# Sum of reciprocals: eight rows of the first 80 computed entirely on ScalarE

## The chip, the cores and the metric

The kernel runs on one core of one Trainium2 chip. The metric is the device time of one execution in microseconds (us). The engines are named as in the profile: PE (TensorE, matmul), DVE (VectorE), ACT (ScalarE), POOL (GpSimd) and SP (SyncE, which here only issues transfers). A profile is of one execution; its span runs from the first to the last instruction of the program.

## The reference

```python
# x: (32, 512, 1024) float32, positive
np.sum(1.0 / x, axis=-1).astype(np.float32)
```

There are 16384 sums of 1024 reciprocals each, over 67.11 MB of input. The output is 64 KB.

## The kernel before

The 16384 sums lie 128 on each of 128 partitions. A "row" r is therefore 128 x 1024 numbers, one sum per partition, 512 KB. Rows 0 to 125 are handled whole; the last two are cut into four half rows, numbered 126 to 129. The rows are loaded into `ring`, which has 40 slots of one row; row r goes into slot r modulo 40, so row r+40 can be loaded only when all readers and writers of row r are done.

The kernel uses 1/a + 1/b = (a + b) / (a b), where a is an element of a row's first half and b the element beside it in the second half. A row thus needs 512 products, 512 reciprocals of products, and a multiply with accumulation. The reciprocal is made on ScalarE as exp(-ln(S a b)), with S = 2^17, which the final multiplication takes out again.

All engines work through one order written out by hand, the list `PLAN` (lines 38 to 73). Each engine runs its own tokens in the order of the list, and each waits only for the data it needs. Semaphore waits come from the recorded reads and writes (`note`, lines 135 to 164). A token is a letter, a row, "+n" for n neighbouring rows, and "@b" for a slot or a bank:

- D n: SP issues the loads of the next n rows (line 187).
- P: POOL multiplies the two halves into `prod`, which has 22 slots of 512 elements (line 199). P0+2 handles two rows in one instruction.
- C and V: for a few rows the product is not POOL's. C copies the row's second half to a PSUM bank through a matmul with the identity (line 209); V multiplies that bank with the first half on DVE (line 220). W is V with both halves from `ring`.
- L: ScalarE takes Ln of the product, in place in `prod` (line 242).
- E: ScalarE takes Exp with scale -1 (line 251). With "@b" the result goes to PSUM bank b, without to `prod` in place.
- S: PE adds the two halves of a row into a PSUM bank, as two accumulating matmuls with the identity (line 232). It is done for about half of the rows, those whose E stays in `prod`.
- R: DVE multiplies and accumulates into the row's column of `sums` (line 267). A row with an S needs 512 elements; a row without needs 1024, its two halves from `ring` against the reciprocal in PSUM. Behind the instruction comes a short one that reads out the accumulator.

A matmul of 32-bit numbers appears in the profile as two passes, two weight loads and two MATMUL instructions.

In the first 80 rows the order repeats with a period of eight rows: POOL makes three pairs of products and a single one, and V makes the eighth, that of row 3, 11, 19, 27, 35, 43, 51, 59, 67 and 75. ScalarE runs L and E on pairs, one instruction of 1024 elements for two rows, alternating Exp to PSUM (banks 6 and 7) and Exp in place. From row 80 on the order is less regular, with many single rows.

When the first 114 sums are all done, they are written out by six transfers (line 289); the rest go out at the end (line 291). One table load at the start (line 84) brings the set that holds both Ln and Exp.

Of the kernel before, what the change touches and what calls it, by code (L numbers as in the profile page):

```python
# [11 lines left out]
def kernel(  # L12
# [5 lines left out]
    nc = tc.nc  # L18
# [5 lines left out]
    R = 40  # L24
    NP = 22
    LAST = F - 2
    DONE = 114
    S = float(2**17)

    PLAN = """
        D2 D10 D14 D14 P0+2 C3@3 S2@0 V3 P2 L0+2@0 C11@3 S3@1 E0+2@6 P4+2 V11 L2+2@2 R0 S6@2
        E2+2 R1 P6+2 L4+2@4 R2 R3 E4+2@6 S7@0 P8+2 L6+2@8 R4 S10@1 E6+2 R5 P10 L8+2@10 R6 R7  # L40
        S11@2 E8+2@6 L10+2@6 R8 E10+2 R9 D11 R10 R11 P12+2 C19@3 S14@0 V19 P14+2 L12+2@12
        S15@1 E12+2@6 S18@2 R12 P16+2 L14+2@16 R13 E14+2 R14 P18 L16+2@18 R15 S19@0 E16+2@6
        P20+2 L18+2@14 R16 S22@1 E18+2 R17 D9 P22+2 L20+2@20 R18 R19 E20+2@6 S23@2 P24+2
        L22+2@0 R20 E22+2 R21 L24+2@2 R22 R23 E24+2@6 P26 C27@3 R24 S26@0 P28+2 V27 R25 D7
        L26+2@4 C35@3 E26+2 S27@1 P30+2 V35 L28+2@8 R26 S30@2 R27 E28+2@6 P32+2 L30+2@10 R28
        S31@0 E30+2 R29 P34 L32+2@12 S34@1 R30 R31 E32+2@6 P36+2 S35@0 L34+2@6 R32 E34+2 R33
        D7 P38+2 S38@2 L36+2@16 R34 R35 E36+2@6 S39@1 P40+2 L38+2@18 R36 C43@3 E38+2 R37 D6
        S42@0 P42 L40+2@14 V43 R38 E40+2@6 P44+2 R39 S43@2 L42+2@20 R40 E42+2 S46@1 R41 D3
        P46+2 L44+2@0 R42 R43 E44+2@6 S47@0 P48+2 L46+2@2 R44 S50@2 E46+2 R45 P50 L48+2@4
        R46 C51@3 R47 E48+2@6 S51@1 P52+2 V51 R48 D6 L50+2@8 C59@3 E50+2 R49 P54+2 S54@0  # L50
        L52+2@10 V59 R50 E52+2@6 R51 S55@2 P56+2 L54+2@12 R52 E54+2 S58@1 R53 D5 P58
        L56+2@16 R54 R55 E56+2@6 S59@0 P60+2 L58+2@6 R56 S62@2 E58+2 R57 D4 P62+2 L60+2@14
        R58 R59 E60+2@6 S63@1 P64+2 L62+2@18 R60 S66@0 E62+2 R61 D4 P66 L64+2@20 R62 C67@3
        R63 E64+2@6 P68+2 S67@2 V67 R64 L66+2@0 S70@1 R65 D4 E66+2 P70+2 L68+2@2 R66 R67
        S71@0 E68+2@6 P72+2 L70+2@4 R68 D3 E70+2 R69 D2 C75@3 P74 L72+2@10 S74@2 R70 V75
        P76+2 E72+2@6 R71 S75@1 L74+2@8 R72 D2 E74+2 R73 D2 P80 S78@0 L76+2@12 R74 P81
        L80@16 R75 S79@2 E76+2@6 P78+2 L81@17 R76 D2 S81@1 E80@5 E81 R80 L78+2@6 W82 E78+2
        R81 R77 D1 D1 D1 D1 D1 P88 C85@6 S85@1 R78 P83 L88@18 V85 E88@7 R79 P84 S84@0
        L82+2@14 R88 E82+2@5 P86+2 L84+2@19 R82 D1 E84+2 R83 D1 D1 D1 C90@7 P91 L86+2@0
        S91@2 R85 P93 V90 E86+2@5 R84 P92 S90@1 L90+2@2 R87 L93@21 W89 L92@10 R86 D1 D1 D1  # L60
        D1 E93@7 P94 S97@0 E92@6 R93 E90+2 P97 S94@3 L89@11 R92 E89@7 P95 L97@8 R91 S95@4
        E97 R90 L94+2@4 W96 R97 P101 C99@6 L96@9 R89 E94+2 S100@0 P98 V99 E96@5 L101@12 R95
        P100 S99@1 L98@13 R96 E101@7 L99+2@16 R101 E98@6 P104 C103@5 R94 E99+2 S105@2 R98
        P102 L104@18 V103 E104@7 W105 L102+2@6 R100 P107+2 C106@6 L105@14 R104 E102+2@4
        S108@0 V106 E105 R102 L106+3@19 P109 S107@3 R103 P110 E106+3 R105 S106@4 R99 P111+2
        L109+2@0 R107 S112@1 R108 E109+2@6 R106 L111+2@10 P114 R109 S111@0 E111+2 R110 P113
        L114@15 R111 C115@7 P116 L113@2 R112 E114@6 V115 E113@5 S117@0 P117 R114 L116@3
        L115@8 P118 E116@7 R113 S118@1 E115@6 P119 L117+2@12 R116 E117+2 R115 P120 S120@2
        L119@9 R117 P121 L120@4 S121@3 R118 E119@7 E120 R119 P122 L121@5 S122@0 E121 R120
        P123 L122@18 R121 E122 W124 L123@6 R122 L124@7 W125 S125@1 E123@7 E124@6 R123 P126  # L70
        L125@14 P127 L126@16 S127@0 R124 E125 P128 L127@17 S128@2 E126@7 P129 R125 E127
        S129@3 L128@19 R126 L129@20 E128 R127 E129 R128 R129
    """.split()

    Ln = mybir.ActivationFunctionType.Ln
    Exp = mybir.ActivationFunctionType.Exp
# [36 lines left out]
    def place(r):  # L113
        if r < LAST:
            return r, 0, H
        part, q = divmod(r - LAST, F - LAST)
        return LAST + q, part * H, H // 2
# [6 lines left out]
    left = set(range(DONE))  # L124
    bank, copied, halves, summed = {}, {}, set(), set()

    history = {}
    begun = {}
    count = {}
# [1 line left out]
    def note(engine, inst, reads=(), writes=()):  # L135
        inst = inst.ins
        known = dict(begun.get(engine, {}))
        before = {}
        for spaces, writing in ((reads, False), (writes, True)):
            for space in spaces:  # L140
                for other in history.get(space, ()):
                    if writing or other[3]:
                        before[other[0].name] = other
        needed = sorted(before.values(), key=lambda o: -o[4])
        for other in needed:
            o_inst, o_engine, o_tick, _, _, o_known = other
            if o_engine == engine:
                continue
            if o_tick <= known.get(o_engine, 0):
                tc.declare_no_dep(inst, o_inst, reason="implied by other waits")  # L150
                continue
            for e, t in o_known.items():
                known[e] = max(known.get(e, 0), t)
            known[o_engine] = max(known.get(o_engine, 0), o_tick)
        count[engine] = count.get(engine, 0) + 1
        begun[engine] = known
        entry = (engine, count[engine])
        if engine == "SP":
            entry = (f"load {count[engine]}", 1)
        for spaces, writing in ((reads, False), (writes, True)):  # L160
            for space in spaces:
                history.setdefault(space, []).append(
                    (inst, *entry, writing, sum(count.values()), known)
                )
# [10 lines left out]
    def slots(r, n):  # L175
        return [("slot", pslot[q]) for q in range(r, r + n)]

    with tc.manual_schedule():
        for op, r, n, b in ops:
# [60 lines left out]
            elif op == "L":  # L240
                pg = prod[:, p : p + n, : place(r)[2]]
                inst = nc.scalar.activation(out=pg, in_=pg, func=Ln, scale=S)  # L242
                note("ACT", inst, writes=slots(r, n))
            elif op == "E":
                pg = prod[:, p : p + n, : place(r)[2]]
                rc = pg
                if b is not None:
                    rc = ps[:, b : b + n, : place(r)[2]]
                    for j in range(n):
                        bank[r + j] = b + j  # L250
                inst = nc.scalar.activation(out=rc, in_=pg, func=Exp, scale=-1.0)  # L251
                if b is None:
                    note("ACT", inst, writes=slots(r, n))
                else:
                    banks = [("bank", b + j) for j in range(n)]
                    note("ACT", inst, slots(r, n), banks)
            elif op == "R":
                q, at, w = place(r)
                other = ps[:, bank[r], :w]
                if r in halves:  # L260
                    row = prod[:, p, :w]
                else:
                    row = ring[:, q % R, at : at + 2 * w]
                    row = row.rearrange("p (h e) -> p h e", h=2)
                    other = other.unsqueeze(1).to_broadcast([P, 2, w])
                total = sums[:, q : q + 1]
                inst = nc.vector.tensor_tensor_reduce(  # L267
                    out=row,
                    in0=row,
                    in1=other,  # L270
                    scale=S,
                    scalar=total if q in summed else 0.0,
                    op0=mult,
                    op1=add,
                    accum_out=total,
                )
                summed.add(q)
                note(
                    "DVE",
                    inst,  # L280
                    [("bank", bank[r])],
                    slots(r, 1) if r in halves else rows(r, 1),
                )

                left.discard(r)
                if not left:
                    for c in range(0, DONE, DONE // 6):
                        part = slice(c, min(c + DONE // 6, DONE))
                        nc.sync.dma_start(out=out_v[:, part], in_=sums[:, part])
                    left.add(-1)  # L290
        nc.sync.dma_start(out=out_v[:, DONE:], in_=sums[:, DONE:])


# [28 lines left out]
```

## Time and profile before

| | us |
|---|---|
| median of 3 runs (168.28 to 168.44) | 168.35 |
| span of the profiled execution | 166.3 |
| what lies around the span, by the median | 2.05 |
| busy in that span: PE | 132.5 |
| busy: ACT | 132.3 |
| busy: DVE | 128.3 |
| busy: POOL | 128.2 |
| one row product on POOL, of a pair (128x1024) / single (128x512) | 2.36 / 1.28 |
| DVE: product 128x512, sum of 128x1024, sum of 128x512 | 0.68, 1.22, 0.68 |
| ACT: Ln or Exp, 128x1024 / 128x512 / 128x256 | 1.05 / 0.62 / 0.40 |

The profile gives no total for the profiled execution other than its span, so the 2.05 us come from the median of the runs. The transfers moved 67.26 MB, 404 GB/s over the span, and up to 441 GB/s in the slices of the first half. Durations are those of single instructions; since the next instruction starts before the last one's end is acknowledged, the distance from start to start ("pitch") is shorter than the duration, unless one needs the other's result. A chain of waits ("the chain that ended last") follows the last instruction back to what released it at each step. Idle time is shown ahead of the instruction that ends it, with what released that one. Instructions of the trace can be matched to tokens, since each engine runs them in the order of `PLAN`.

### The profile page before, as it was taken

The numbers are of one execution on the slowest core, as the hardware profiler recorded it, in microseconds if no ns is written. First come the engines' busy times: TensorE is split into PE (matmuls) and PEld (weight loads), VectorE is DVE, ScalarE is ACT, GpSimd is POOL, SyncE is SP. The second block draws the span as 40 slices with busy tenths as digits, with TensorE's granted clock in tenths as the row PEclk, the third lists the DMA queues.
The fourth block names the chain that finished last, engine by engine and source line by source line (L and its number), as shares of the span: only waits on it lengthen the run. The fifth ranks groups of instructions, "written<-read, shape, count | busy, mean of one in ns | idle before, by whom it ended". The sixth has DMA issues, their size and how long they took to land.

```text
span 166.3 us, 1348 instructions
## 1 busy us (share of the span) xinstructions
PE 132.5 (80%) x292; PEld 55.2 (33%) x292; DVE 128.3 (77%) x282; ACT 132.3 (80%) x157; POOL 128.2 (77%) x81
## 2 busy tenths in 40 slices
PE   0000799978855999999999999988699979989982
PEld 0000333333312444444343433324234424433351
DVE  0000119885787699898998898989899999999994
ACT  3040073949995899999799999996999999999992
POOL 1500795069995999999999999948977869999860
PEclk9999999999996999999999999999999999999999
DMA  5999999999998989999999999999999999999940
GB/s 189 536 394 394 441 441 441 441 441 441 441 441 349 509 368 446 430 417 438 441 434 434 406 426 446 429 424 424 414 437 437 414 410 428 410 409 410 400 139 4
DMA packets 5768, 67.26 MB, mean 404 GB/s; under 512 B 1536, under 2 KB 1536, under 8 KB 3200
## 3 DMA queue, kind: packets, MB, share of 16 engines
q1 hardware_dynamic: 5760, 67.18, 95.6%
q8 instruction: 2, 0.03, 0.1%
q14 instruction: 6, 0.05, 0.1%
HBM read 67.11 MB, written 0.07 MB: 404 GB/s over the span
## 4 chain that ended last, share of the span: by engine, by line
DMA 57%; PE 18%; ACT 8%; DVE 6%; POOL 6%; issue 3%; SPq 1%; ACTq 0%; POOLq 0%; DVEq 0%
DMA ring<-in_x_dram 57%; PE ps L232 15%; POOL prod L199 6%; ACT prod L242 4%; PE ps L209 3%; ACT ps L251 2%; DVE ring L267 2%; DVE prod L267 2%; ACT prod L251 2%; DVE prod L220 1%; SPq L187 1%; DVE sums L267 0%; ACTq L242 0%; POOLq L199 0%; DVEq L317 0%
## 5 line engine op out<-in xcount | busy, mean ns | idle before, releaser
L199 POOL TENSOR_TENSOR prod<-ring 128x1024 f32<-128x1024 f32 (+2 forms) x75 | 127.5, 1727 | 33.5 <-DMA ring<-in_x_dram 27.1
L232 PE MATMUL ps<-ring,ident 128*128 128x512 f32 (+1 forms) x260 | 116.9, 596 | 5.2 <-DVE sums L267 4.5
L242 ACT ACTIVATE prod<-prod 128x1024 f32<-128x1024 f32 (+2 forms) x78 | 68.5, 892 | 24.9 <-DVE prod L220 14.3
L267 DVE CUSTOM_DVE_ANT_1 ring<-ring,ps 128x1024 f32<-128x1024 f32 (+1 forms) x65 | 76.4, 1208 | 8.9 <-ACT ps L251 8.7
L232 PEld LDWEIGHTS ps<-ring,ident 128*128 128x128 f32 x260 | 49.2, 193 | 71.7 <-issue 51.6
L267 DVE CUSTOM_DVE_ANT_0 prod<-prod,ps 128x512 f32<-128x512 f32 (+1 forms) x63 | 40.9, 677 | 0.4 <-PE ps L232 0.4
L209 PE MATMUL ps<-ring,ident 128*128 128x512 f32 x32 | 19.3, 689 | 25.7 <-DMA ring<-in_x_dram 24.0
L251 ACT ACTIVATE ps<-prod 128x1024 f32<-128x1024 f32 (+2 forms) x41 | 34.1, 838 | 4.5 <-DVE sums L267 3.7
L251 ACT ACTIVATE prod<-prod 128x1024 f32<-128x1024 f32 (+3 forms) x37 | 34.4, 931 | 0.9
L220 DVE TENSOR_TENSOR prod<-ring,ps 128x512 f32<-128x512 f32 x16 | 10.9, 684 | 26.3 <-PE ps L209 26.3
L209 PEld LDWEIGHTS ps<-ring,ident 128*128 128x128 f32 x32 | 6.0, 213 | 36.0 <-issue 21.4
L267 DVE DVE_READ_ACCUMULATOR2_ANT sums<- 128x1 f32 x130 | 10.7, 82 | 0.0
L220 DVE TENSOR_TENSOR prod<-ring 128x512 f32<-128x512 f32 x6 | 4.1, 688 | 0.1
L84 ACT ACT_TABLE_LOAD x1 | 1.3, 1283 | 0.7 <-PEq L306 0.7
L267 DVE CUSTOM_DVE_ANT_0 prod<-prod,ps,sums 128x256 f32<-128x256 f32 x2 | 0.9, 475 | 0.0
masks.py:197 POOL MEMSET ident<- 128x128 f32 x1 | 0.2, 204 | 0.3 <-POOLq L306 0.3
masks.py:199 POOL TENSOR_SCALAR_AFFINE_SELECT ident<-ident 128x128 f32<-128x128 f32 x1 | 0.3, 292 | 0.1
L306 POOL MEMSET const-float32-0.0<- 128x1 f32 x1 | 0.1, 98 | 0.2 <-issue 0.2
L306 POOL MEMSET const-bfloat16-1.0<- 128x1 bf16 x1 | 0.1, 101 | 0.0
L306 POOL MEMSET const-uint8-127<- 128x1 uint8 x1 | 0.1, 101 | 0.0
L306 POOL MEMSET const-float32-1.0<- 128x1 f32 x1 | 0.1, 98 | 0.0
## 6 DMA issues: line engine op xcount, KB each, us to landing
ring<-in_x_dram SPq DMA_DIRECT2D x2, 7168.0 KB, 41.2
ring<-in_x_dram SPq DMA_DIRECT2D x2, 3584.0 KB, 29.3
ring<-in_x_dram SPq DMA_DIRECT2D x2, 3072.0 KB, 31.9
ring<-in_x_dram SPq DMA_DIRECT2D x3, 2048.0 KB, 34.0
ring<-in_x_dram SPq DMA_DIRECT2D x1, 5632.0 KB, 30.3
ring<-in_x_dram SPq DMA_DIRECT2D x5, 1024.0 KB, 31.8
ring<-in_x_dram SPq DMA_DIRECT2D x1, 5120.0 KB, 16.5
ring<-in_x_dram SPq DMA_DIRECT2D x1, 4608.0 KB, 30.7
```

The lines of the kernel that those rows point to most:

```text
L84: nc.scalar.add_instruction(mybir.InstLoadActFuncSet(name=nc.get_next_instruction_name(), act_func_set_id=act_sets.index("natural_log_exp_ ...
L187: inst = nc.sync.dma_start(out=ring[:, a : a + m, at : at + 2 * w], in_=x_v[:, q : q + m, at : at + 2 * w],)
L199: inst = nc.gpsimd.tensor_tensor(out=prod[:, p : p + m, :w], in0=ring[:, a : a + m, at : at + w], in1=ring[:, a : a + m, at + w : at + 2 * w],
L209: inst = nc.tensor.matmul(ps[:, b, : place(r)[2]], lhsT=ident, rhs=xs(r, 1), start=True, stop=True,)
L220: inst = nc.vector.tensor_tensor(out=prod[:, p, :w], in0=xs(r, 0), in1=in1, op=mult)
L232: inst = nc.tensor.matmul(ps[:, b, : place(r)[2]], lhsT=ident, rhs=xs(r, h), start=h == 0, stop=h == 1,)
L242: inst = nc.scalar.activation(out=pg, in_=pg, func=Ln, scale=S)
L251: inst = nc.scalar.activation(out=rc, in_=pg, func=Exp, scale=-1.0)
L267: inst = nc.vector.tensor_tensor_reduce(out=row, in0=row, in1=other, scale=S, scalar=total if q in summed else 0.0, op0=mult, op1=add, acc ...
L306: nc = _bacc.Bacc("TRN2", target_bir_lowering=False, num_devices=1)
```

## The change

Rows 11, 19, 27, 35, 43, 51, 59 and 67 get two new tokens on ScalarE. A takes Ln of the row's 1024 elements, in place in its ring slot. Z takes Exp with scale -1 of the same 1024 elements, in place, with an accumulated sum (`accum_out`) into the row's column of `sums`. For these rows C, S, V and R are dropped (eight of each). The L and E of the pair that such a row was in become instructions of one row; A and Z stand right behind that E. The remaining tokens and their order, and those of the loads, stay as they were. Four of the eight replacements in the order:

```
C11@3 ... V11 ... S11@2 E8+2@6 L10+2@6 R8 E10+2 R9 D11 R10 R11
    -> E8+2@6 L10@6 R8 E10 A11 Z11 R9 D11 R10
C19@3 ... V19 ... S19@0 ... L18+2@14 R16 S22@1 E18+2 R17 ... R18 R19
    -> L18@14 R16 S22@1 E18 A19 Z19 R17 ... R18
V27 R25 D7 L26+2@4 C35@3 E26+2 S27@1 P30+2 ... R26 ... R27
    -> R25 D7 L26@4 E26 A27 Z27 P30+2 ... R26
S67@2 V67 R64 L66+2@0 S70@1 R65 D4 E66+2 P70+2 ... R66 R67
    -> R64 L66@0 S70@1 R65 D4 E66 A67 Z67 P70+2 ... R66
```

The rest of the diff, its core:

```diff
         for other in needed:
             o_inst, o_engine, o_tick, _, _, o_known = other
-            if o_engine == engine:
-                continue
             if o_tick <= known.get(o_engine, 0):
                 tc.declare_no_dep(inst, o_inst, reason="implied by other waits")
+                continue
+            if o_engine == engine:
                 continue
...
+            elif op == "A":
+                q, at, w = place(r)
+                row = ring[:, q % R, at : at + 2 * w]
+                inst = nc.scalar.activation(out=row, in_=row, func=Ln)
+                note("ACT", inst, writes=rows(r, 1))
+            elif op == "Z":
+                q, at, w = place(r)
+                row = ring[:, q % R, at : at + 2 * w]
+                inst = nc.scalar.activation(
+                    out=row,
+                    in_=row,
+                    func=Exp,
+                    scale=-1.0,
+                    accum_out=sums[:, q : q + 1],
+                )
+                summed.add(q)
+                note("ACT", inst, writes=rows(r, 1) + [("sum", q)])
+                left.discard(r)
...
-                    slots(r, 1) if r in halves else rows(r, 1),
-                )
-
+                    (slots(r, 1) if r in halves else rows(r, 1)) + [("sum", q)],
+                )
                 left.discard(r)
-                if not left:
-                    ...
+            if not left:
+                ...
```

The first part of it lets a dependency on an earlier instruction of the same engine be declared as implied where other waits already cover it. The last part records which column of `sums` an R writes, and moves the test for the first 114 sums out of R's branch, so that a Z can be the last of them too.

More of the change, by code (lines that the diff above doesn't have):

```diff
@@ L38 @@
     PLAN = """
[L39 to L72, printed above, removed]
+        D2 D10 D14 D14 P0+2 C3@3 S2@0 V3 P2 L0+2@0 S3@1 E0+2@6 P4+2 L2+2@2 R0 S6@2 E2+2 R1 P6+2
+        L4+2@4 R2 R3 E4+2@6 S7@0 P8+2 L6+2@8 R4 S10@1 E6+2 R5 P10 L8+2@10 R6 R7 E8+2@6 L10@6 R8
@@ new lines @@
+        E10 A11 Z11 R9 D11 R10 P12+2 S14@0 P14+2 L12+2@12 S15@1 E12+2@6 S18@2 R12 P16+2 L14+2@16
+        R13 E14+2 R14 P18 L16+2@18 R15 E16+2@6 P20+2 L18@14 R16 S22@1 E18 A19 Z19 R17 D9 P22+2
+        L20+2@20 R18 E20+2@6 S23@2 P24+2 L22+2@0 R20 E22+2 R21 L24+2@2 R22 R23 E24+2@6 P26 R24
+        S26@0 P28+2 R25 D7 L26@4 E26 A27 Z27 P30+2 L28+2@8 R26 S30@2 E28+2@6 P32+2 L30+2@10 R28
+        S31@0 E30+2 R29 P34 L32+2@12 S34@1 R30 R31 E32+2@6 P36+2 L34@6 R32 E34 A35 Z35 R33 D7
+        P38+2 S38@2 L36+2@16 R34 E36+2@6 S39@1 P40+2 L38+2@18 R36 E38+2 R37 D6 S42@0 P42
@@ new lines @@
+        L40+2@14 R38 E40+2@6 P44+2 R39 L42@20 R40 E42 A43 Z43 S46@1 R41 D3 P46+2 L44+2@0 R42
+        E44+2@6 S47@0 P48+2 L46+2@2 R44 S50@2 E46+2 R45 P50 L48+2@4 R46 R47 E48+2@6 P52+2 R48 D6
+        L50@8 E50 A51 Z51 R49 P54+2 S54@0 L52+2@10 R50 E52+2@6 S55@2 P56+2 L54+2@12 R52 E54+2
+        S58@1 R53 D5 P58 L56+2@16 R54 R55 E56+2@6 P60+2 L58@6 R56 S62@2 E58 A59 Z59 R57 D4 P62+2
+        L60+2@14 R58 E60+2@6 S63@1 P64+2 L62+2@18 R60 S66@0 E62+2 R61 D4 P66 L64+2@20 R62 R63
+        E64+2@6 P68+2 R64 L66@0 S70@1 R65 D4 E66 A67 Z67 P70+2 L68+2@2 R66 S71@0 E68+2@6 P72+2
@@ new lines @@
+        L70+2@4 R68 D3 E70+2 R69 D2 C75@3 P74 L72+2@10 S74@2 R70 V75 P76+2 E72+2@6 R71 S75@1
+        L74+2@8 R72 D2 E74+2 R73 D2 P80 S78@0 L76+2@12 R74 P81 L80@16 R75 S79@2 E76+2@6 P78+2
+        L81@17 R76 D2 S81@1 E80@5 E81 R80 L78+2@6 W82 E78+2 R81 R77 D1 D1 D1 D1 D1 P88 C85@6
+        S85@1 R78 P83 L88@18 V85 E88@7 R79 P84 S84@0 L82+2@14 R88 E82+2@5 P86+2 L84+2@19 R82 D1
+        E84+2 R83 D1 D1 D1 C90@7 P91 L86+2@0 S91@2 R85 P93 V90 E86+2@5 R84 P92 S90@1 L90+2@2 R87
+        L93@21 W89 L92@10 R86 D1 D1 D1 D1 E93@7 P94 S97@0 E92@6 R93 E90+2 P97 S94@3 L89@11 R92
@@ new lines @@
+        E89@7 P95 L97@8 R91 S95@4 E97 R90 L94+2@4 W96 R97 P101 C99@6 L96@9 R89 E94+2 S100@0 P98
+        V99 E96@5 L101@12 R95 P100 S99@1 L98@13 R96 E101@7 L99+2@16 R101 E98@6 P104 C103@5 R94
+        E99+2 S105@2 R98 P102 L104@18 V103 E104@7 W105 L102+2@6 R100 P107+2 C106@6 L105@14 R104
+        E102+2@4 S108@0 V106 E105 R102 L106+3@19 P109 S107@3 R103 P110 E106+3 R105 S106@4 R99
+        P111+2 L109+2@0 R107 S112@1 R108 E109+2@6 R106 L111+2@10 P114 R109 S111@0 E111+2 R110
+        P113 L114@15 R111 C115@7 P116 L113@2 R112 E114@6 V115 E113@5 S117@0 P117 R114 L116@3
@@ L73 @@
+        L115@8 P118 E116@7 R113 S118@1 E115@6 P119 L117+2@12 R116 E117+2 R115 P120 S120@2 L119@9
+        R117 P121 L120@4 S121@3 R118 E119@7 E120 R119 P122 L121@5 S122@0 E121 R120 P123 L122@18
+        R121 E122 W124 L123@6 R122 L124@7 W125 S125@1 E123@7 E124@6 R123 P126 L125@14 P127
+        L126@16 S127@0 R124 E125 P128 L127@17 S128@2 E126@7 P129 R125 E127 S129@3 L128@19 R126
+        L129@20 E128 R127 E129 R128 R129
     """.split()
@@ L281 @@
                     [("bank", bank[r])],
-                    slots(r, 1) if r in halves else rows(r, 1),
+                    (slots(r, 1) if r in halves else rows(r, 1)) + [("sum", q)],
                 )
                 left.discard(r)
-                if not left:
[L287 to L290, printed above, removed]
+            if not left:
+                for c in range(0, DONE, DONE // 6):
+                    part = slice(c, min(c + DONE // 6, DONE))
+                    nc.sync.dma_start(out=out_v[:, part], in_=sums[:, part])
+                left.add(-1)
         nc.sync.dma_start(out=out_v[:, DONE:], in_=sums[:, DONE:])
```

## The prediction

> **What bounds the kernel now.** I read the page first, then the busy time by stage, then the instructions of ScalarE in order of time, then the waits of the stages. Two lines of the page, shares of the span by engine and the chain that ended last:
>
> ```profile
> PE 132.5 (80%) x292; PEld 55.2 (33%) x292; DVE 128.3 (77%) x282; ACT 132.3 (80%) x157; POOL 128.2 (77%) x81
> ...
> DMA 57%; PE 18%; ACT 8%; DVE 6%; POOL 6%; issue 3%; SPq 1%; ACTq 0%; POOLq 0%; DVEq 0%
> ```
>
> The averages separate nothing, and the chain gives the loads 57%, so stages are needed. The busy time by stage cuts at 54.50 (row 26 begins on ScalarE), 98.57 (row 68 begins) and 163.30 (ScalarE's last end); columns are busy us and (count) for PE, weight loads, DVE, ACT and POOL, then TensorE clock, DMA share, GB/s. The third line is DVE's last stretch, from the sum of row 76 (R76) to its last sum:
>
> ```profile
> 54.50:98.57 44.07, 43.62 (x102) 18.54 (x100) 39.78 (x86) 42.28 (x42) 43.98 (x22) 1.00 0.99 424
> 98.57:163.30 64.73, 58.43 (x136) 24.46 (x134) 62.33 (x140) 62.17 (x89) 53.68 (x40) 1.00 0.95 393
> 109.22:164.02 54.80, 48.28 (x114) 20.53 (x112) 53.93 (x120) 51.65 (x77) 43.40 (x34) 1.00 0.93 383
> ```
>
> From 54.50 on ScalarE is busy 42.28 of 44.07 us and then 62.17 of 64.73: every stretch that it gains or loses is felt. DVE is at 90% in the first stage and at 53.93 of 54.80 in its last. Who ScalarE waits for, after 54 us, and DVE, after 109 (total us, times, longest):
>
> ```profile
> ACT prod L242 <- DVE prod L220: 3.8, 4, 2.4
> ACT prod L242 <- POOL prod L199: 1.6, 2, 1.3
> ```
>
> ```profile
> DVE ring L267 <- ACT ps L251: 1.5, 2, 0.8
> ```
>
> The instructions of ScalarE in order of time (start, duration) give the pitches used below: the first four lines are a pair L26+2, E26+2, then L28+2, E28+2; the last are single rows (L121, E121, L122, E122):
>
> ```profile
> 54.50 1.06 ACT L242 ACTIVATE prod<-prod 128x1024 f32<-128x1024 f32 x1 [2.44 <-DVE prod L220]
> 55.59 1.06 ACT L251 ACTIVATE prod<-prod 128x1024 f32<-128x1024 f32 x1
> 56.55 1.04 ACT L242 ACTIVATE prod<-prod 128x1024 f32<-128x1024 f32 x1
> 57.62 1.03 ACT L251 ACTIVATE ps<-prod 128x1024 f32<-128x1024 f32 x1
> ...
> 155.27 0.62 ACT L242 ACTIVATE prod<-prod 128x512 f32<-128x512 f32 x1
> 155.92 0.63 ACT L251 ACTIVATE prod<-prod 128x512 f32<-128x512 f32 x1
> 156.46 0.61 ACT L242 ACTIVATE prod<-prod 128x512 f32<-128x512 f32 x1
> 157.10 0.63 ACT L251 ACTIVATE prod<-prod 128x512 f32<-128x512 f32 x1
> ```
>
> An instruction that needs the one before it starts 1.08 later at 1024 elements and 0.65 at 512; one that does not, 0.96 and 0.54 later.
>
> **Part 1, what is removed beside the path.** Per special row one copy (C, one product of two PE passes), one half sum (S, two such), one product and one sum on DVE go. In the chain 28 passes take 12.02 us, 0.43 each, so PE gives back 6 x 0.43 = 2.6 us a row. On DVE a product and a half-row sum have a pitch of 0.60 and 0.61, so 1.2 us a row. I price both at nothing in themselves: between 54.50 and 98.57 the only idle time of ScalarE is ended by DVE's product, never by a sum, so an earlier sum releases nobody. The chain's 18% on PE runs from 51.6 to 79.1 and ends in just such a product. POOL keeps its 75 products (2.35 a pair, 1.28 a single) and was ahead of ScalarE all along (P26 ends at 52.97 before L26 at 54.50, P66 at 94.12 before L66 at 96.52). If POOL's lead were gone, ScalarE would lose up to the 1.5 to 2.4 us of it; but a slower ScalarE lengthens it.
>
> **Part 2, waits that vanish.** L26, L50 and L66 waited for the product on DVE of their second row, 2.44, 0.83 and 0.29 us; without it L50 and L66 give back their 1.12 us. L26 is worked out with the start, next.
>
> **Part 3, ScalarE's new work.** Before, a pair costs 1.08 + 0.96 = 2.04. After, its place holds L (0.65 to E), E (0.54 to A), A of 1024 (1.08 to Z, which needs it) and Z of 1024 (0.96 to the next): 3.23, so +1.19 a special row. In place on the ring, A and Z have the shape of the prod<-prod 128x1024 rows, 1.06 us. What no row of the trace shows is Z's accumulated sum on ScalarE. From below: DVE's sums come with an accumulator read of 82 ns that starts together with the next instruction, so it adds 0 to the pitch. From above: ScalarE's smallest instructions, 128x256, have a pitch of 0.31. I take 0.15, half of that: less than 256 elements' time, but ScalarE need not hide it as DVE does. So 1.34 a special row, between 1.19 and 1.50. By the page "ScalarE: Activation LUTs" of the Trainium skill (section What ACT_TABLE_LOAD costs) an activation takes 186 ns + 0.833 ns per element and overlaps the next by 93 ns. An estimate from this, with one element, is 0.09 for the read and 1.28 a row, which would lower the sum by 0.4. Tables add nothing: Ln and Exp alternate already behind a single load.
>
> **Part 4, by rows.** Row 11 is hidden: ScalarE then waits until P12 ends at 37.05 (2.39 idle), and without V11 it gets to rows 4 to 10 earlier. Row 19: L18 stays at 43.78; E18 44.43, A19 44.97, Z19 46.05, L20 47.16 (was 45.82), then three pairs of 2.04, so L26 at 53.29, past P26's end of 52.97: 1.21 earlier than 54.50. The idle 2.44 has paid for row 19 and gives 1.21 besides. Then six rows (27, 35, 43, 51, 59, 67) at 1.34 add 8.04. ScalarE starts L68 later by 8.04 - 1.21 - 1.12 = **5.7 us** (4.8 with the lower price, 6.7 with the upper).
>
> **Part 5, what is given back.** After row 68 the program is the same, and so a delay can only shrink. ScalarE's recoverable idle there is 2.0 (1.34 before L88, the rest in pieces of 0.09 to 0.25). DVE has less: R76 waits for E76 (0.83), so it starts late by the whole 5.7, and from there to its end DVE idles 54.80 - 53.93 = 0.87. The saving of part 1 on DVE lies ahead of R76, where it waits for ScalarE; it can't be carried over. So the last sum ends 5.7 - 0.9 = **4.8 us** later, between 3.9 and 5.8.
>
> **Part 6, the loads.** Row 51's slot is now freed by Z11, and so on. The chain view shows the cover:
>
> ```profile
> 2.11 49.45 DMA ring<-in_x_dram
> ...
> 101.96 35.20 DMA ring<-in_x_dram
> ```
>
> The first four loads land by 51.56, while the fifth is issued at 35.13: 16 us early, the least lead of the loads that wait for a slot. The one issued at 101.96 lands at 137.16, behind a queue. Slots come at most some 6 us later, so the stream doesn't run dry; price nothing, and beyond 16 us one for one. The other edit, which drops waits of an engine on itself that other waits imply, also counts nothing: no stall in the views is ended by the engine itself.
>
> **Sum.** The profiled execution has a span of 166.3 us; the median of the runs is 168.35, so 2.05 lie around the span, kept as they are. Span 166.3 + 4.8 = 171.1; time 168.35 + 4.8 = **173.2 us**; bounds 172.2 to 174.2.
>
> **A rule for the change, weighed.** DVE's 90% against ScalarE's 96% in the stage that is changed says that the work moves to the fuller engine. The Trainium skill, "Perfetto Trace Analysis", section Optimizing Scalar/DVE Operations, says that with DVE saturated, offloading some work to Scalar may make sense. Here its condition fails by those rows; by the rule the sums above would come out as a gain of up to the 1.2 us a row, 7 us of DVE, which no wait in that stage asks for.
>
> **The rivals.**
> 1. *The stream sets the end (not slower).* If the late stage is paced by the loads alone, the delay is swallowed and the time stays at 168.3. For it: DMA 57% of the chain, DMA share 0.99, and P123 starts at 156.22 on the heels of its load. A pair costs ScalarE 2.04 where the stream gives two rows in 2.4. Against: it decides only if both ScalarE and DVE have 5.7 us to give after row 68, and they have 2.0 and 0.9. The Trainium skill, "Perfetto Trace Analysis", section Roofline, calls elementwise work memory-bound at almost any intensity, with some 435 GB/s for a core's 16 DMA engines. By that rule the time would not move; 424 GB/s between 54 and 99 agrees on the bandwidth, the full ScalarE speaks against the conclusion. 5%.
> 2. *ScalarE's idle is what counts, and the accumulated sum is free.* 4.8 - 2.0 = 2.8 later, 171.1. It needs DVE to have 2 us of hidden slack; 0.87 says no. 8%.
> 3. *Z and the sums on DVE hold each other up,* since both write the tile of sums: each Z waits for the sum then running on DVE, up to its 1.22, half on average. 6 x 0.61 = 3.7 more: 176.9. The code gives the columns separately, and the trace has no such pair of writers. 9%.
>
> That the eight rows are not really moved can't be: their tokens are gone from the order.
>
> **How the numbers follow.** Forecast 173.2: 78%; rivals 5, 8 and 9%. The range reaches from just above rival 2 to some way towards rival 3, 171.9 to 175.2, leaving out rival 1, rival 3 and most of rival 2. A difference of 0.2%, 0.34 us, is about what a measurement of this kernel can tell from none. Faster 0.02, same 0.03 (rival 1 splits), slower 0.95.
>
> **What would show it.** After: ScalarE without a gap from L26 at about 53.3 to the end; busy time up by about 8 x (1.19 to 1.5) = 10 to 12 us, to 142 to 144; L68 near 104.3; PE busy about 20 and DVE about 10 lower; DVE waiting for ScalarE in the first 100 us; R76 to the end nearly unbroken, near 54 us; loads landing as before. It would be wrong if the last stage took under 53 us from R76 on, if ScalarE waited for DVE after row 68, or if Z were far from 1.06 us.

## The result, and the profile after

The changed kernel takes 177.16 us (176.38 to 177.89) against 168.39 us in the same measurement: slower, ratio 1.0526 (95% interval 1.048 to 1.0572). I had forecast slower, 173.2 us with 175.2 at most; 177.16 lies outside. Its runs fall at two levels, 176.4 and 177.9 us; the profile is of a run of 176.47, with a span of 174.7, and what adds 1.4 us in the others no trace here shows.

Two lines of the page, busy time by engine and the chain that ended last:

```profile
PE 120.6 (69%) x244; PEld 48.4 (28%) x244; DVE 122.3 (70%) x258; ACT 141.7 (81%) x181; POOL 129.2 (74%) x81
...
DVE 37%; ACT 26%; DMA 19%; issue 12%; POOL 4%; SPq 0%; DVEq 0%
```

ScalarE has 9.4 us more work and PE 11.9 less, but DVE only 6.0 less, where by the pitches of part 1 8 x 1.21 = 9.7 had been taken off it. The chain no longer rests on the loads: DVE and ScalarE carry 63% of it. The stages, cut at the same instructions as before (L26 to L68, L68 to ScalarE's last end, then R76 to the last sum):

```profile
53.14:103.53 50.39, 36.51 (x67) 13.41 (x66) 35.81 (x76) 49.53 (x61) 49.79 (x25) 0.87 0.99 425
103.53:171.21 67.68, 59.14 (x134) 25.11 (x134) 64.72 (x134) 61.98 (x90) 50.24 (x37) 0.97 0.84 346
114.18:171.94 57.76, 49.38 (x114) 21.16 (x112) 57.75 (x120) 51.46 (x77) 42.14 (x32) 0.97 0.80 326
```

In the first stage ScalarE has no gap (49.53 of 50.39; the rest is 0.03 us ahead of each dependent instruction). In the last line DVE is busy all the time, 57.75 of 57.76, but that is 3.8 us more than the 53.93 which the same instructions needed before. Who waits, on ScalarE after 54 us and on DVE after 113:

```profile
ACT ps L236 <- DVE sums L270: 3.2, 2, 2.8
ACT prod L227 <- DVE prod L205: 1.6, 3, 1.0
ACT prod L227 <- POOL prod L184: 0.3, 1, 0.3
```

```profile
DVE ring L270 <- ACT ps L236: 0.8, 1, 0.8
```

ScalarE now waits for DVE in the late stage, by my own list a sign that I am wrong. The instructions of ScalarE show what a special row costs (L26, E26, A27, Z27, the read of the accumulator, L28):

```profile
53.14 0.61 ACT L227 ACTIVATE prod<-prod 128x512 f32<-128x512 f32 x1
53.78 0.63 ACT L236 ACTIVATE prod<-prod 128x512 f32<-128x512 f32 x1
54.32 1.04 ACT L245 ACTIVATE ring<-ring 128x1024 f32<-128x1024 f32 x1
55.39 1.06 ACT L250 ACTIVATE ring<-ring 128x1024 f32<-128x1024 f32 x1
56.36 0.19 ACT L250 ACTIVATION_READ_ACCUMULATOR ring<-ring 128x1 f32 x1
56.45 1.04 ACT L227 ACTIVATE prod<-prod 128x1024 f32<-128x1024 f32 x1
```

The read of the accumulator is an instruction of its own, 186 ns long, but L28 starts 0.09 us behind it. L26 to L28 is 3.31 where a pair takes 2.04, 1.27 a row. L68 starts at 103.53, 4.96 later than before.

Then the part that I had not seen. The products on DVE, grouped by what they read (count, then minimum, median and maximum in ns, then first and last start), before and after:

```profile
L220 DVE TENSOR_TENSOR prod<-ring,ps x16: 679/684/689, 19.9 to 148.4; 128x512 f32<-128x512 f32 x16
L220 DVE TENSOR_TENSOR prod<-ring x6: 681/688/693, 111.5 to 158.7; 128x512 f32<-128x512 f32 x6
```

```profile
L205 DVE TENSOR_TENSOR prod<-ring,ps x8: 676/678/689, 19.9 to 156.6; 128x512 f32<-128x512 f32 x8
L205 DVE TENSOR_TENSOR prod<-ring x6: 686/978/2826, 116.5 to 166.5; 128x512 f32<-128x512 f32 x6
```

The products with both halves from the ring (the W tokens) took 0.69 us each before; now one takes 2.83. Its place on DVE, and POOL at the same time:

```profile
116.47 2.83 DVE L205 TENSOR_TENSOR prod<-ring 128x512 f32<-128x512 f32 x1
119.22 0.67 DVE L270 CUSTOM_DVE_ANT_0 prod<-prod,ps 128x512 f32<-128x512 f32 x1
```

```profile
116.39 2.35 POOL L184 TENSOR_TENSOR prod<-ring 128x1024 f32<-128x1024 f32 x1
```

W82 starts 0.08 us after POOL's P86+2 and ends at 119.30, 0.55 us after P86+2's end at 118.74. The three others in the middle do the same: W89 ends at 130.39 (P101 at 129.84), W96 at 135.68 (P104 at 135.13), W105 at 145.42 (P111+2 at 144.87), each 0.55 later. Before, five of the six W lay in gaps of POOL, and W124 met only the last 0.13 us of P123, at no cost. W82, for instance, ran from 111.51 to 112.20, between P78+2 (to 110.06) and P88 (from 112.85):

```profile
111.51 0.69 DVE L220 TENSOR_TENSOR prod<-ring 128x512 f32<-128x512 f32 x1
```

```profile
107.69 2.37 POOL L199 TENSOR_TENSOR prod<-ring 128x1024 f32<-128x1024 f32 x1
112.85 1.27 POOL L199 TENSOR_TENSOR prod<-ring 128x512 f32<-128x512 f32 x1 [2.79 <-DVE sums L267]
```

(The view puts P88's wait down to a sum on DVE that ended at that moment; by the order P88 needs no such sum, but its load, which landed at 112.72.) POOL follows the loads, whose landings have hardly moved (row 129 at 161.53, before 161.27); DVE follows ScalarE and came 5 us later. So the W slid out of POOL's gaps and into its products.

The sum, against the profiled spans: L68 later by 4.96; the W longer by 2.14, 0.55, 0.04 and 1.55, together 4.28; idle time of DVE given back, 1.33, taken from start to start (0.73 of it ahead of R82, where the view shows 0.64); so the last sum ends 7.91 later (171.93 against 164.02). The closing of the program behind the last store's landing takes 1.33 us instead of 0.86. 7.91 + 0.47 = 8.4 = 174.7 - 166.3.

### The profile page after: what moved, and what is told of

Same layout as the page of the kernel before. It is cut to its first block, busy times and chain, and to the rows that moved or that the text cites. A ratio compares the mean times of both kernels' runs of the same rounds, so it can differ in the third digit from the quotient of the medians.

```text
span 174.7 us, 1233 instructions
## 1 busy us (share of the span) xinstructions
PE 120.6 (69%) x244; PEld 48.4 (28%) x244; DVE 122.3 (70%) x258; ACT 141.7 (81%) x181; POOL 129.2 (74%) x81
## 4 chain that ended last, share of the span: by engine, by line
DVE 37%; ACT 26%; DMA 19%; issue 12%; POOL 4%; SPq 0%; DVEq 0%
DVE ring L270 20%; DMA ring<-in_x_dram 19%; DVE prod L270 10%; ACT ps L236 9%; ACT prod L227 8%; DVE prod L205 5%; POOL prod L184 4%; ACT ring L245 4%; ACT prod L236 3%; ACT ring L250 2%; DVE sums L270 1%; SPq L172 0%; DVEq L319 0%
## 5 line engine op out<-in xcount | busy, mean ns | idle before, releaser
L217 PE MATMUL ps<-ring,ident 128*128 128x512 f32 (+1 forms) x228 | 112.8, 645 | 30.7 <-DVE sums L270 22.9
L227 ACT ACTIVATE prod<-prod 128x1024 f32<-128x1024 f32 (+2 forms) x78 | 65.0, 846 | 23.7 <-DVE prod L205 12.2
L217 PEld LDWEIGHTS ps<-ring,ident 128*128 128x128 f32 x228 | 45.5, 207 | 98.3 <-issue 52.4
L270 DVE CUSTOM_DVE_ANT_0 prod<-prod,ps 128x512 f32<-128x512 f32 (+1 forms) x55 | 35.9, 676 | 0.9 <-PE ps L217 0.9
L236 ACT ACTIVATE prod<-prod 128x1024 f32<-128x1024 f32 (+3 forms) x37 | 31.0, 840 | 0.9
L194 PE MATMUL ps<-ring,ident 128*128 128x512 f32 x16 | 9.5, 675 | 18.2 <-DMA ring<-in_x_dram 17.8
L205 DVE TENSOR_TENSOR prod<-ring,ps 128x512 f32<-128x512 f32 x8 | 5.4, 680 | 19.9 <-PE ps L194 19.9
L194 PEld LDWEIGHTS ps<-ring,ident 128*128 128x128 f32 x16 | 2.9, 204 | 22.4 <-issue 19.7
L250 ACT ACTIVATE ring<-ring 128x1024 f32<-128x1024 f32 x8 | 8.5, 1057 | 0.3
L205 DVE TENSOR_TENSOR prod<-ring 128x512 f32<-128x512 f32 x6 | 8.4, 1397 | 0.0
L245 ACT ACTIVATE ring<-ring 128x1024 f32<-128x1024 f32 x8 | 8.3, 1040 | 0.0
L250 ACT ACTIVATION_READ_ACCUMULATOR ring<-ring 128x1 f32 x8 | 1.5, 186 | 0.0
```

Source lines behind the costliest of these rows:

```text
L194: inst = nc.tensor.matmul(ps[:, b, : place(r)[2]], lhsT=ident, rhs=xs(r, 1), start=True, stop=True,)
L205: inst = nc.vector.tensor_tensor(out=prod[:, p, :w], in0=xs(r, 0), in1=in1, op=mult)
L217: inst = nc.tensor.matmul(ps[:, b, : place(r)[2]], lhsT=ident, rhs=xs(r, h), start=h == 0, stop=h == 1,)
L245: inst = nc.scalar.activation(out=row, in_=row, func=Ln)
L250: inst = nc.scalar.activation(out=row, in_=row, func=Exp, scale=-1.0, accum_out=sums[:, q : q + 1],)
L270: inst = nc.vector.tensor_tensor_reduce(out=row, in0=row, in1=other, scale=S, scalar=total if q in summed else 0.0, op0=mult, op1=add, acc ...
```

## The experiments

Theory 1: ScalarE's added time delays DVE against POOL, and the rest of the loss is DVE's two-ring products held up by POOL's. Its rivals: the loss is ScalarE's and the long W are a symptom; the work spared on PE and DVE matters; the other edits matter. The kernel before, measured beside each group of them, took 168.24 to 168.28 us by its medians.

**1. The four W from PSUM.** In the changed kernel:

```diff
-S81@1   ... W82  ... S91@2 ... W89  ... S97@0 ... W96  ... C103@5 ... W105
+S81@1 C82@3 ... V82 ... S91@2 C89@3 ... V89 ... S97@0 C96@5 ... V96 ... C103@5 C105@4 ... V105
```

> The changed kernel, but DVE's four products with both halves from the ring in the middle of the late stage (W82, W89, W96, W105) read their second half from a PSUM bank, copied by PE (C and V in place of W). Theory 1, DVE's two-ring product and a POOL product do not run beside each other: in the changed kernel these four took 2.83, 1.23, 0.73 and 2.23 us where 0.69 is usual; from PSUM they take 0.68 each. L68 still starts 4.96 us later than in the kernel before, DVE gives back its 0.88 of idle time, the last sum ends 4.1 us later, time 168.4 + 4.1 = 172.5 us (172.0 to 173.0). Theory 2, the longer time comes from ScalarE's late stage or from the sums, and the long products are a symptom of waits: they stay long or their time turns up elsewhere, 176 to 178 us.

Measured 173.52 us, ratio 1.0304 (1.0279 to 1.0329). All four take 0.69 us and the long ones have gone: theory 1 in kind. It is 0.5 us above my 173.0; in the profile V82 waited 1.32 us for its copy, which PE had to make behind S81, and experiment 2 takes that wait away.

**2. The same, copy of row 82 earlier.** `S79@2 C82@3` instead of `S81@1 C82@3`:

> The changed kernel with W82, W89, W96 and W105 read from PSUM as before, but the copy of row 82 stands one half sum earlier on PE (C82 ahead of S81). In the run with the later copy V82 waited 1.32 us for PE, and the last sum was 5.06 us later than in the kernel before. Theory 1: without that wait the remainder of my sum is left, 4.96 - 0.64 - 0.24 = 4.1 us on the last sum, 172.3 to 172.8 us. Theory 2: the 5.06 are the price of ScalarE's work and the wait was idle anyway: 173.5 us as before.

Measured 173.07 us (172.76 to 173.40), ratio 1.0286 (1.0272 to 1.03). The products now read (minimum, median, maximum in ns; the two left are W124 and W125):

```profile
L208 DVE TENSOR_TENSOR prod<-ring,ps x12: 680/682/690, 19.9 to 152.8; 128x512 f32<-128x512 f32 x12
L208 DVE TENSOR_TENSOR prod<-ring x2: 678/722/766, 161.5 to 162.8; 128x512 f32<-128x512 f32 x2
```

L68 starts 5.00 later, R82 4.72, the last sum 4.19: 5.00 less the 0.87 of part 5 is 4.13, so that part's sum holds within 0.1 once the collisions are gone. The median is 0.3 above the expected interval, of which the longer closing (0.48) is the reason I can name. Against theory 2, the last sum ends 0.87 us earlier than in experiment 1, so the wait of V82 had cost time; that is by one profile of each, and the medians differ by 0.45 us with intervals that overlap.

**3. The kernel before, with the same four from PSUM.**

> The kernel before, with the same four products read from PSUM. In that kernel each of them lies in a gap of POOL and takes 0.69 us. Theory 1: nothing to gain, 168.4 us (168.2 to 168.8), PE busy up by 4 x 0.86 = 3.4 us. Theory 2 (the copy through PE has a price or a gain of its own): different from 168.4 by over 0.5 us, which would then also be in the run of the changed kernel with PSUM.

Measured 168.47 us, ratio 1.0017 (1.0001 to 1.0034); PE busy 135.8 against 132.5. Where the W met no product of POOL, moving them gains nothing.

**4. Collisions without any added work.** In the kernel before, two tokens of DVE change places:

```diff
-L90+2@2 R87 L93@21 W89 L92@10
+L90+2@2 W89 R87 L93@21 L92@10
```

> The kernel before with one token moved: W89 ahead of R87 instead of behind it on DVE. No work is added. W89 then starts at about 121.65, inside POOL's P92 (121.40 to 122.68). Theory 1: W89 ends 0.55 us after P92, at 123.2, DVE is 0.98 us late; W96 then starts at 129.0 inside P101 (128.71 to 129.99) and ends near 130.5, 0.9 us more; W105 starts near 138.1 inside P107+2 (137.29 to 139.66) and ends near 140.2, 1.5 us more. DVE has 0.2 us of idle time left, so the last sum is some 3 us later: 171.5 us (170.5 to 172.5). Theory 2: a swap of two independent instructions on DVE costs nothing, 168.4 us.

Measured 172.48 us (171.03 to 172.81), ratio 1.023 (1.0182 to 1.0278). W89 on DVE, and POOL's P92, which began before it:

```profile
121.71 1.57 DVE L222 TENSOR_TENSOR prod<-ring 128x512 f32<-128x512 f32 x1
123.20 1.21 DVE L269 CUSTOM_DVE_ANT_1 ring<-ring,ps 128x1024 f32<-128x1024 f32 x1
```

```profile
121.45 1.28 POOL L201 TENSOR_TENSOR prod<-ring 128x512 f32<-128x512 f32 x1
```

W89 ends 0.55 after P92. It makes W96 late (1.62 us), that W105 (2.14), and W124, which I had not foreseen, takes 1.27. The four together are 3.85 us longer, each moving DVE into the next one, and DVE also waits 1.2 us for half sums of PE, where it waited for none in that stretch before. The last sum is 4.73 us later, with the same instructions in the kernel.

**5. ScalarE's time alone.** In the kernel before, six tokens stand twice (E28+2@6, E36+2@6, E44+2@6, E52+2@6, E60+2@6, E64+2@6), the second writing what the first wrote:

> The kernel before, with six of ScalarE's instructions issued twice, the second writing the same values again (E28, E36, E44, E52, E60, E64 to PSUM): ScalarE's work between row 28 and row 68 grows by 6 x 0.96 to 1.07 = 5.8 to 6.4 us, and nothing is taken off PE or DVE. Theory 1 (ScalarE's added time is the whole of the first part, and what PE and DVE are spared is worth nothing): the waits for V51 and V67 (1.12 us) are swallowed, L68 starts 4.6 to 5.3 us later, and behind it the same kind of collisions of DVE's products with POOL's: 174.5 to 178 us. Theory 2 (the work taken off PE and DVE does pay, so that without it the delay is larger): L68 later by over 6 us, or 178 us and more.

In the profile L68 starts 4.92 later, in the interval of theory 1, though DVE and PE were spared nothing. From L28 on, both kernels add the same time to ScalarE (5 rows x 1.27 = 6.4 us in the changed kernel, 6 x 1.06 = 6.4 here); from there to L68 the delay grows by 5.06 in the changed kernel and by 5.43 here, so what was spared is worth at most 0.4 us. W82, W89, W96 and W105 take 2.64, 1.58, 1.58 and 1.02 us, and the last sum is 7.68 us later, the changed kernel's 7.91 all but reproduced:

```profile
L222 DVE TENSOR_TENSOR prod<-ring,ps x16: 676/684/687, 19.8 to 156.4; 128x512 f32<-128x512 f32 x16
L222 DVE TENSOR_TENSOR prod<-ring x6: 689/1296/2644, 116.4 to 166.3; 128x512 f32<-128x512 f32 x6
```

The times were 175.77, 175.63, 175.78 and once 172.49, outside the 174.5 to 178 of theory 1; there is no ratio from times so far apart, and the profile is of the 175.77. In it W82 starts at 116.44 and P86+2 at 116.19, a quarter of a microsecond earlier. That W82 came first in the run of 172.49 would fit, but that run has no profile, so it is not shown.

**6. Only row 82 from PSUM.** `C82@3` behind `S79@2` and V82 for W82, in the changed kernel:

> The changed kernel with only row 82's product read from PSUM; W89, W96 and W105 stay as they are. Theory 1 (each collision depends on where DVE stands against POOL at that moment, and an earlier one shifts the later ones): without W82's 2.14 us DVE comes to W89 about 1.6 us earlier, at 127.5, in a gap of POOL (P95 ends at 127.45, P101 begins at 128.57), so W89 takes 0.69; W96 then starts near 132.75, at the end of P100 (to 132.76), 0.55 to 0.7; W105 near 140.9 inside P109 (139.96 to 141.24), ends near 141.8, 0.2 to 0.3 more. Time 172.9 to 173.7 us, hardly more than with all four moved (173.07). Theory 2 (each of the four adds its own excess): only 2.1 us of the 4.3 are saved, 174.6 us or more.

Measured 172.92 us (172.79 to 173.21), ratio 1.027 (1.0254 to 1.0286), as theory 1 had it: moving one W does what moving four did. W89, W96 and W105 take 0.83, 0.68 and 0.88 us with nothing done to them. The 4.28 us are no sum of four independent prices; W82's 2.14 brought the others on.

**7. The four products on POOL.** In the changed kernel, W82, W89, W96 and W105 become P82, P89, P96 and P105, behind P78+2, P92, P95 and P102:

> The changed kernel with the products of rows 82, 89, 96 and 105 made by POOL in its gaps, not by DVE. DVE's late stage is 4 x 0.60 = 2.4 us shorter. Theory 1: DVE's delay at R76 (4.96) shrinks by 0.88 idle and 2.4 to 1.7; ScalarE's delay shrinks by its own idle of 2.0 only, so now ScalarE sets the end, 3.0 to 3.5 us later: 171.2 to 171.9 us. Theory 2 (DVE alone sets the end): 170.1 us. Theory 3 (the collisions were not it): 176 us.

Measured 171.39 us, ratio 1.0184 (1.0171 to 1.0197), as theory 1 had it. ScalarE from L68 to its last end, and DVE from R76 to its last sum:

```profile
103.55:166.19 62.64, 58.12 (x134) 24.12 (x134) 58.77 (x130) 61.69 (x90) 55.19 (x41) 1.00 0.91 376
114.20:166.92 52.72, 48.65 (x114) 20.36 (x112) 51.80 (x116) 51.16 (x77) 45.85 (x35) 1.00 0.88 360
```

ScalarE is full (61.69 of 62.64) and its last end is 2.89 later than before, 4.98 less its 2.1 of idle time. So this is about what the eight rows cost when next to nothing collides (W124 takes 0.83) and DVE has room.

**8. The same four on POOL in the kernel before.**

> The kernel before with the same four products made by POOL. DVE is 2.4 us shorter behind 109 us, ScalarE has 2.0 us of idle time, but the last loads land at 161.3 us as before and the last rows follow them. Theory 1: nearly nothing, 167.6 to 168.4 us. Theory 2 (the late stage is bound by DVE alone and the loads have room): 166.0 us.

Measured 168.92 us, ratio 1.0041 (1.0028 to 1.0053): neither theory, slightly slower. The loads land 0.4 us later in this run (row 88 at 113.11 against 112.72, row 129 at 161.64 against 161.27), P88 and the last sum are each 0.39 later with them. Why the loads came later stays open. DVE's 2.4 us bought nothing.

**9. Three rows only.** The changed kernel up to Z27, then the order of the kernel before, without R27:

> Only rows 11, 19 and 27 are done whole on ScalarE, rows 35, 43, 51, 59 and 67 as in the kernel before. In the changed kernel L28 starts at 56.45, 0.10 us earlier than before, since the three rows' work fills the idle time ahead of L12 and L26. Theory 1 (ScalarE's added time counts only where ScalarE has no idle time): the whole loss is gone, 168.0 to 168.6 us. Theory 2 (each such row costs its share, whatever stands idle): three eighths of 8.8 us, 171.7 us.

Measured 168.61 us, ratio 1.0018 (1.0009 to 1.0027). L28 starts 0.05 later than in the kernel before, the last sum ends 0.06 later. So the first three rows alone are free, and the loss comes with the other five. ScalarE's waits from 54 us on:

```profile
ACT prod L231 <- POOL prod L188: 2.1, 4, 1.5
ACT prod L231 <- DVE prod L209: 1.0, 3, 0.4
```

But for the 2.44 ahead of L26, which are gone, they stand about where they stood, with 1.5 ahead of L88: of the 0.46 by which L50 was earlier, 0.25 are left at L88, behind row 88's load. DVE loses these at W89, which now starts 0.25 earlier, inside P92, and takes 1.09: one collision, of which the last sum shows 0.06.

**10. The bookkeeping edit alone.**

> The kernel before with only the edit to the dependency bookkeeping: dependencies of an engine on itself that other waits imply are declared as such. Theory 1 (no stall in the profile is ended by the engine itself): nothing, 168.2 to 168.4 us. Theory 2 (the edit changes the queues or the closing of the program): over 0.3 us either way. In the changed kernel the closing behind the last store's landing takes 1.33 us against 0.86; if it takes 1.3 here too, the edit is what lengthens it.

Measured 168.50 us, ratio 1.0018 (1.0006 to 1.0031), 0.1 above my 168.4; the last sum is 0.11 us later, the closing 0.86. By the medians this edit explains at most 0.3 of the 8.8 us, and nothing of the longer closing. Here too W89 started earlier, inside P92, and took 1.07: in the kernel before it starts only 0.11 us after P92's end, so little is needed for the two to meet. The closing is 1.33 or 1.34 us in the kernels with eight special rows (the changed one, experiments 1, 2, 6 and 7), 1.10 with three rows and 0.85 or 0.86 with none; what lengthens it stays open.

No version beat the kernel before.

## Why the prediction was wrong, step by step

- **Part 1 held.** The work spared on PE and DVE is worth at most 0.4 us in the first stage: with none of it spared, experiment 5, by its one profile, has nearly the same delay for the same ScalarE time. PE's busy time fell by 11.9 us and not by about 20, because the passes that are left took longer (those of the half sums 645 ns on average against 596); after 53 us neither DVE nor ScalarE waited for one.
- **Parts 2 to 4 held.** L26 started 1.36 earlier (I had 1.21), a special row costs 1.27 (1.34), L68 is 4.96 late (5.7, bounds 4.8 to 6.7). Two terms were mis-sized: the read of the accumulator has 0.09 of pitch, not 0.15, and the waits ahead of L50 and L66 gave back 1.26 from start to start, not the 1.12 that the views count as idle. With these, 6 x 1.27 - 1.36 - 1.26 = 5.0. The estimate of 0.09 from the page "ScalarE: Activation LUTs" of the Trainium skill (section What ACT_TABLE_LOAD costs) agrees with the trace.
- **Part 5 failed, at the sentence "After row 68 the program is the same, and so a delay can only shrink".** That would hold if all engines were delayed together, and DVE's stretch from R76 on would have been near 54 us; it was 57.8. POOL is paced by the loads and stays where it was. DVE and ScalarE slide along it by 5 us, and four of the six products that DVE makes with both halves from the ring ran into POOL's. The trace of before held the clue: the W lie in POOL's gaps. I priced a product on DVE by its duration, 0.69, without asking what stood beside it. 4.28 us are missing in the sum for this, and 0.47 for the closing; 0.46 more idle time was given back than the 0.87 I had, which the views count short of what it is from start to start. Experiment 2 takes the collisions away and leaves the 4.1 to 4.2 us of the rest of the part.
- **A page had the rule.** The Trainium skill, "SBUF — State Buffer", section Who interferes with whom, states that a DVE instruction with two SBUF inputs contends with a GpSimd instruction that reads SBUF. By its section Summary: rules for kernel authors the second to issue fully blocks until the first finishes. The 0.55 us from POOL's end to W's end in four cases, and the unchanged 0.68 of products with one half in PSUM, agree with it.
- **Part 6 held.** No load lands more than 0.3 us later than before.
- **The rivals.** Rival 1 is refuted by the result. Rival 2 (171.1) was refuted for this kernel, but is about what experiment 7 measures (171.39) once DVE has room. Rival 3 asked for sums that hold each other up: Z never waits for DVE. The case that came, a delay that drives two engines' instructions into each other, was not among my rivals, and so my upper end had no room for it.

## What to carry to other kernels

Ask of each delay which engines take part in it and which keep their own clock: a delay moves the one group against the other, and a pair of instructions that never met before may meet after. Where two engines' instructions hold each other up, as these did, the price of an instruction is its duration only in a gap of the other engine, so the gaps belong in the sum. Here ScalarE's work was free as long as it filled ScalarE's own waits (three rows), and delayed what stands behind it beyond that.

## What the runs showed of the hardware

A DVE product with both inputs in the ring that starts inside a POOL product, and more than 0.14 us before its end, ends 0.55 us after it (0.54 or 0.55 in all 18 such cases of the twelve traces), whether it started 0.08 us after POOL did or 1.10 (W96); the POOL product next in line is held in turn (P98 and P102 take 1.73 us, P110 in experiment 6 too, where 1.28 is usual). ScalarE's accumulated sum costs 0.09 us of its time. PE, busy for 36.51 of 50.39 us in the first stage, was granted a clock of 0.87 there where it had 1.00 when nearly full; after 53 us neither DVE nor ScalarE waited for PE. The lower clock is not the loss: in experiment 5 that stage had a clock of 1.00 and L68 came as late.
